# A two-layer hybrid trunk: another order of the seven products in a unit of the up-projections, and the recurrent gates as two steps

## The chip, the cores and the metric

The kernel runs on one core of a Trainium2 chip. The metric is the time of one execution in microseconds of device time; lower is better.

## The reference

1040 tokens (16 learned ones and 1024 of the input) of width 1024 pass through two layers; all of it is float32. Cut to what matters:

```python
def short_conv_mixer(x, w_in, conv_w, w_out):
    h = jnp.einsum('btd,de->bte', x, w_in)            # 1024 -> 3 * 1024
    b_gate, c_gate, v = jnp.split(h, 3, axis=-1)
    u = causal_dwconv(c_gate * v, conv_w)
    return jnp.einsum('btd,de->bte', b_gate * u, w_out)

def rglru_block(x, w_in, conv_w, conv_b, w_gate_a, b_gate_a, w_gate_x, b_gate_x, lam, w_out):
    h = jnp.einsum('btd,de->bte', x, w_in)            # 1024 -> 2 * 1280
    g_branch, r_branch = jnp.split(h, 2, axis=-1)
    gate = jax.nn.gelu(g_branch, approximate=True)
    u = causal_dwconv(r_branch, conv_w) + conv_b      # width 4
    ub = u.reshape(bsz, t_len, RG_BLOCKS, RG_BLOCK_DIM)   # 10 blocks of 128
    r = jax.nn.sigmoid(jnp.einsum('btki,kij->btkj', ub, w_gate_a)... + b_gate_a)
    i = jax.nn.sigmoid(jnp.einsum('btki,kij->btkj', ub, w_gate_x)... + b_gate_x)
    log_a = -RG_C * r * jax.nn.softplus(-lam)
    a = jnp.exp(log_a)
    b = jnp.sqrt(-jnp.expm1(2.0 * log_a)) * (i * u)
    _, hs = lax.associative_scan(_lin_rec_combine, (a, b), axis=1)   # h = a * h + b
    return jnp.einsum('bte,ed->btd', hs * gate, w_out)

def conv_gated_mlp(x, w_up, conv_w, w_down):          # 1024 -> 2 * 2816 -> 1024
    g, v = jnp.split(causal_dwconv(jnp.einsum('btd,df->btf', x, w_up), conv_w), 2, axis=-1)
    return jnp.einsum('btf,fd->btd', jax.nn.silu(g) * v, w_down)

# layer 0: h += short_conv_mixer(rms_norm(h));  h += conv_gated_mlp(rms_norm(h))
# layer 1: h += rglru_block(rms_norm(h));       h += conv_gated_mlp(rms_norm(h))
# out = rms_norm(h)[:, 16:]
```

## The kernel before, in words

Activations lie with the channel in the partitions and the 1040 tokens along the free axis. There are four stages, each an up-projection (`up`) and a down-projection (`down`): the short convolution (sc_w_in, sc_w_out), the first MLP (ffn0), the recurrent block (rg_w_in, rg_w_out) and the second MLP (ffn1). In the profile's span they begin near 0, 391, 1101 and 1483 us; the down-projections begin near 264, 826, 1333 and 1916.

Each float32 operand is split into a high and a low part (`whi`, `wlo` for weights, made by a cast on ACT, L227, and a subtraction on DVE, L228; `zh`, `zl` for the down-projections' activations, L522 and L523), and three products of parts stand for one.

An up-projection works in units. A unit gives two blocks of 128 output channels for all tokens. One unit (two in sc_w_in) is *plain* (L418). Each other one is made in the manner of Strassen and Winograd, of seven products (`product`, L445) of 24 matmuls each, 128 x 128 by 128 x 260, which add up in three banks: bank a takes 1, 6, 7 and 4 one after the other, bank b takes 2, bank c takes 5 and 3. All of PSUM is one pool of four such tiles (`banks`). As a bank is only read between two products that follow each other in it, `take` copies or adds out what it then holds: ACT copies after 1 (L461), 6 (L465), 7 (L468) and 4 (L471), DVE adds after 2 (L463), 7 (L469) and 3 (L473). A product that goes into a bank waits for the copy of the one before it there.

`unit_order` is the hand-written order of TensorE: in a unit 2, 6, 5, 7, then 1 of the next unit (written 1' below), then 4 and 3. After a unit, `finish` does the elementwise part. In the recurrent stage `rg_finish` (one unit is one of the ten blocks) multiplies by the norm (L774, L778) and convolves: an Identity on ACT (L776) and three fused steps on DVE (L624), which give the tile `u`.

The gates of block i (`gates`) run on TensorE one unit later, behind product 3 of unit i + 1: four PSUM tiles, two for the gate `ra` and two for `ix` (L791; each tile is two matmul instructions, and four records in the trace), each followed by a sigmoid on ACT (L794). Then, in the order of the text: GpSimd multiplies ix by u (L795), ACT does tanh (L796), exp (L797), square (L798), sqrt (L800) and gelu (L802), with a table load on ACT wherever the function's table changes, and DVE does L799, L803, the scan (L804) and the product with the gelu (L805), which goes to DRAM (`zrg`). The gates of the last block stand in rg_w_out, after its first pair of output blocks. rg_w_out reads the spilled rows back (`bring`, issued from GpSimd), casts them (L522) and subtracts (L523); DVE evicts its banks at L566.

The order on TensorE and on the DMA queues is that of the code; on ACT and DVE a scheduler with a model of its own sets it, where `tc.high_priority` favours the copies and the sigmoids. Weights are loaded nine pieces and made six pieces ahead of the product that uses them.

## Time and profile before

| | |
|---|---|
| Median of three runs | 2179.39 us (2178.82, 2179.39, 2184.06) |
| The profiled execution | 2182.36 us; its span 2180.5 us |
| TensorE (PE) busy | 2121.6 us, 97% of the span, 17364 matmul records |
| DVE (VectorE) busy | 1489.8 us, 68% |
| ACT (ScalarE) busy | 999.5 us, 46% |
| GpSimd (POOL) busy | 163.5 us, 7% |
| Mean granted clock of TensorE | 0.991 |

All times in the sections below are us from the start of the span. A row of a timeline gives the start, the duration, the engine, the line and the operation, `out<-in`, the sizes, and how many were joined; in brackets the idle time before it and what ended that.

### The profile page before, as it was taken

How to read it: one execution, taken by the hardware profiler on the slowest of the kernel's cores; microseconds unless marked ns; L12 is line 12 of the kernel's file. 1: busy time of each engine (PE TensorE's matmuls, PEld its weight loads, DVE VectorE, ACT ScalarE, POOL GpSimd, SP SyncE). 2: the span in 40 equal slices, each digit the busy share in tenths (PEclk: the TensorE clock that was granted, in tenths of full speed). 3: DMA queues.
4: the chain of work that ended last, by engine and by line, in shares of the span. 5: the costliest groups of instructions: out<-in, count | busy, mean ns of one | idle time of the engine just before them, and what ended most of it. 6: DMA issues, size and time to landing. Idle time of an engine off the chain costs nothing. (4 is left out here: it accounts for less than half of the span.)

```text
span 2180.5 us, 41094 instructions
## 1 busy us (share of the span) xinstructions
PE 2121.6 (97%) x17364; PEld 2108.4 (97%) x17364; DVE 1489.8 (68%) x1858; ACT 999.5 (46%) x1437; POOL 163.5 (7%) x254
## 2 busy tenths in 40 slices
PE   8999999899999999999999999899999999999998
PEld 8999999899999999999989999899999999999997
DVE  8866745887877886233868777497778778763227
ACT  8433433544444444122558788274444444442113
POOL 0000000000000001100001112100000000011002
PEclk9999999999999999999999999999999999999999
DMA  5344454254444446542323345632444444465212
GB/s 179 102 117 113 148 156 118 69 131 117 116 118 120 120 140 205 125 107 65 103 66 93 102 110 151 146 127 68 135 117 114 119 116 122 133 208 148 68 35 78
DMA packets 99545, 257.60 MB, mean 118 GB/s; under 512 B 11040, under 2 KB 19104, under 8 KB 99360
## 3 DMA queue, kind: packets, MB, share of 16 engines
q1 hardware_dynamic: 76320, 172.52, 24.1%
q0 software_dynamic: 22320, 81.73, 18.2%
q8 instruction: 136, 2.23, 0.4%
q10 hardware_dynamic: 720, 0.73, 0.1%
q14 instruction: 49, 0.40, 0.1%
HBM read 205.20 MB, written 49.73 MB: 117 GB/s over the span
## 5 line engine op out<-in xcount | busy, mean ns | idle before, releaser
L445 PE MATMUL ps<-x,whi 128*128 128x260 f32 (+1 forms) x6832 | 1241.7, 284 | 16.6 <-ACT cin L468 8.7
L445 PEld LDWEIGHTS ps<-x,whi 128*128 128x128 f32 x6832 | 1061.9, 190 | 18.7 <-ACT cin L468 9.5
L445 PE MATMUL ps<-x,wlo 128*128 128x260 f32 (+1 forms) x3416 | 969.2, 284 | 0.0
L445 PEld LDWEIGHTS ps<-x,wlo 128*128 128x128 f32 x3416 | 647.5, 190 | 0.0
L556 PE MATMUL ps<-zh,whi 128*128 128x260 f32 (+2 forms) x1888 | 536.1, 284 | 11.4 <-DVE h L566 11.0
L556 PE MATMUL ps<-zl,whi 128*128 128x260 f32 (+2 forms) x1888 | 534.7, 283 | 0.9 <-DVE zl L523 0.9
L556 PE MATMUL ps<-zh,wlo 128*128 128x260 f32 (+2 forms) x1888 | 534.4, 283 | 0.0
L228 DVE TENSOR_TENSOR wlo<-wraw,whi 128x512 fp32r<-128x512 f32 (+1 forms) x337 | 224.8, 671 | 364.7 <-ACT whi L227 364.4
L227 ACT CAST whi<-wraw 128x512 fp32r<-128x512 f32 (+1 forms) x337 | 203.4, 606 | 587.4 <-PE ps L556 347.1
L556 PEld LDWEIGHTS ps<-zh,whi 128*128 128x128 f32 x1888 | 358.2, 190 | 12.8 <-DVE h L566 7.7
L556 PEld LDWEIGHTS ps<-zl,whi 128*128 128x128 f32 x1888 | 358.5, 190 | 1.1 <-DVE zl L523 1.1
L556 PEld LDWEIGHTS ps<-zh,wlo 128*128 128x128 f32 x1888 | 358.2, 190 | 0.0
L227 ACT CAST whi<-s 128x512 fp32r<-128x512 f32 x244 | 150.4, 618 | 258.6 <-PE ps L445 190.2
L624 DVE SCALAR_TENSOR_TENSOR t<-cin,cv,t 128x1040 f32<-128x1040 f32 (+1 forms) x176 | 216.7, 1288 | 5.0 <-ACT t L743 3.3
L228 DVE TENSOR_TENSOR wlo<-s,whi 128x512 fp32r<-128x512 f32 x244 | 166.3, 686 | 44.6 <-ACT whi L227 44.0
L261 POOL DMA_DIRECT2D s<-in_ws x61 | 53.0, 868 | 1241.5 <-DVE cin L740 515.3
L743 ACT ACTIVATE t<-cin,cv 128x1040 f32<-128x1040 f32 (+1 forms) x88 | 97.7, 1152 | 75.5 <-DVE cin L740 75.3
L418 PE MATMUL ps<-x,whi 128*128 128x260 f32 (+1 forms) x640 | 117.1, 285 | 9.2 <-ACT whi L227 9.2
L418 PEld LDWEIGHTS ps<-x,whi 128*128 128x128 f32 x640 | 99.9, 191 | 9.3 <-ACT whi L227 9.2
L740 DVE SCALAR_TENSOR_TENSOR cin<-cin,rn 128x1040 f32<-128x1040 f32 (+1 forms) x88 | 108.1, 1231 | 0.0
L418 PE MATMUL ps<-x,wlo 128*128 128x260 f32 (+1 forms) x320 | 91.1, 285 | 0.1
L463 DVE TENSOR_TENSOR cin<-ps,cin 128x520 f32<-128x520 f32 (+1 forms) x51 | 35.6, 698 | 63.8 <-PE ps L445 63.8
(132 smaller groups left out, 1823.5 us busy)
## 6 DMA issues: line engine op xcount, KB each, us to landing
wraw<-in_ws SPq DMA_DIRECT2D x317, 256.0 KB, 3.5
s<-in_ws SPq DMA_DIRECT2D x61, 512.0 KB, 3.7
s<-in_ws POOLq DMA_DIRECT2D x61, 512.0 KB, 5.7
zff<-t SPq DMA_DIRECT2D x22, 520.0 KB, 2.7
zff<-t SPq DMA_DIRECT2D x22, 512.0 KB, 2.7
h<-h SPq DMA_DIRECT2D x16, 520.0 KB, 2.7
s<-zff POOLq DMA_DIRECT2D x15, 520.0 KB, 4.6
s<-zff POOLq DMA_DIRECT2D x15, 512.0 KB, 4.4
```

The source lines that it names most:

```text
L227: nc.scalar.copy(hi[:, :n], src)
L228: nc.vector.tensor_sub(lo[:, :n], src, hi[:, :n].bitcast(FP32))
L261: nc.gpsimd.dma_start(st["s13"][:, :2 * C], block(q)[:, C:3 * C], accum_op=ALU.add)
L418: nc.tensor.matmul(ps[:, s, :n], lhsT=wt, rhs=x[:, t], start=(j == 0 and k == 0), stop=(j == NJ - 1 and k == 5),)
L445: nc.tensor.matmul(ps[:, b, :n], lhsT=wt[:, c], rhs=x[:, t], start=(first and j == 0 and r == 0), stop=(last and j == NJ - 1 and r == 2), ...
L463: nc.vector.tensor_add(quarter(0, 0), gb, quarter(0, 0))
L556: nc.tensor.matmul(ps[:, s, :n], lhsT=w[wt][:, k], rhs=x[:, t], start=(i == 0 and q == 0), stop=(i == k1 - 1 and q == 2),)
L624: nc.vector.scalar_tensor_tensor(t[:, a:e], cin[:, a + s:e + s], col(wname, at + k), t[:, a:e], op0=ALU.mult, op1=ALU.add)
L740: nc.vector.scalar_tensor_tensor(c, c, sign, rn[:, a:e], op0=ALU.mult, op1=ALU.mult)
L743: nc.scalar.activation(t[:, oa:], cin[:, oa + 2:e + 2], AF.Copy, scale=col(wconv, at + 2))
```

## The change

Three things. `unit_order` becomes 6, 2, 5, 7, 1', 3, 4 (in the first unit 1, 2, 6, 5, 1', 7, 3, 4), so that two products of other banks stand between each pair that follow in bank a. `take` copies bank c after product 5, on ACT, and adds bank a to it after 7, on DVE, where it copied a and added c, both after 7. And the gates of block i become two steps: the one for ra (q = 0) after product 7 of unit i + 1, the one for ix (q = 1) after product 4, followed by `recur`, the elementwise rest as before. The gates of the last block stand after the first and the third pair of rg_w_out.

```diff
 def unit_order(u0, n):
-    out = [(u0, 1)]
+    out = [(u0, 1), (u0, 2)]
     for u in range(u0, n):
-        out += [(u, p) for p in (2, 6, 5, 7)]
-        if u < n - 1:
-            out.append((u + 1, 1))
-        out += [(u, p) for p in (4, 3)]
+        for p in (6, 5, None, 7, 3, 4) if u == u0 else (6, 2, 5, 7, None, 3, 4):
+            if p is not None:
+                out.append((u, p))
+            elif u < n - 1:
+                out.append((u + 1, 1))
     return out
...
             elif p == 6:
                 nc.scalar.copy(quarter(0, 1), ga)
+            elif p == 5:
+                outs[u].append(new_out(u, 1))
+                nc.scalar.copy(quarter(1, 1), gc)
             elif p == 7:
-                outs[u].append(new_out(u, 1))
-                nc.scalar.copy(quarter(1, 1), ga)
-                nc.vector.tensor_add(quarter(1, 1), gc, quarter(1, 1))
+                nc.vector.tensor_add(quarter(1, 1), ga, quarter(1, 1))
...
                 for v in range(n_plain):
-                    between(v)
                     hook(lambda v=v: finish_unit(v))
-            if p == 3:
-                between(u)
+            if p in (7, 4):
+                between(u, p)
+            if p == 4:
                 hook(lambda u=u: finish_unit(u))
...
-    def gates(i, w):
-        u, g = rg.pop(i)
+    def gate(i, q, w):
         n = ALL[1]
-        ra, ix, th = row("ra"), row("ix"), row("th")
-        for q, (bias, got) in enumerate((("b_a", ra), ("b_x", ix))):
-            c = slice(q * P, (q + 1) * P)
-            for b in range(2):
-                ps = banks()
+        u, got = rg[i][0], row(("ra", "ix")[q])
+        rg[i] += (got,)
+        c = slice(q * P, (q + 1) * P)
+        for b in range(2):
+            ps = banks()
...
+        if q:
+            recur(i)
+
+    def recur(i):
+        u, g, ra, ix = rg.pop(i)
+        th = row("th")
         nc.gpsimd.tensor_mul(ix, ix, u)
         nc.scalar.activation(th, ra, AF.Tanh, scale=sp8[:, i:i + 1])
...
+    def gates_between(u, p):
+        add_gate(u - 1, 0 if p == 7 else 1)
+
+    def gates_after(g, m):
+        if g == 0 and m == 0:
+            add_gate(NR - 1, 0)
+        if g == 0 and m == 2:
+            add_gate(NR - 1, 1)
```

The change adds lines, so a line above 70 stands one to seven higher after it (L791 becomes L792, L794 becomes L795, L624 becomes L626). In the lists below the tiles carry the program's numbers, `ps` is a bank, and what an instruction waits for stands in brackets.

**TensorE, at the gates of a steady unit.** Before, behind product 3: four tiles in a row, and the next unit's product 6.

```order
L445 MATMUL ps_13429<-x_12246,wlo_13401 128x260
L791 MATMUL ps_13594<-u_13362,wgate_13325 128x260 [waits DMAHW0_49,PE_49]
L791 MATMUL ps_13594<-u_13362,wgate_13325 128x260
L791 MATMUL ps_13598<-u_13362,wgate_13325 128x260 [waits Activation_49]
L791 MATMUL ps_13598<-u_13362,wgate_13325 128x260
L791 MATMUL ps_13602<-u_13362,wgate_13325 128x260 [waits DVE_49]
L791 MATMUL ps_13602<-u_13362,wgate_13325 128x260
L791 MATMUL ps_13606<-u_13362,wgate_13325 128x260 [waits Activation_49]
L791 MATMUL ps_13606<-u_13362,wgate_13325 128x260
L445 MATMUL ps_13634<-x_11633,whi_13454 128x260 [waits Activation_49]
```

After, behind product 7: the two tiles of ra, and then product 1 of the next unit.

```order
L446 MATMUL ps_13252<-x_12288,wlo_13281 128x260
L792 MATMUL ps_13495<-u_13358,wgate_13228 128x260 [waits DMAHW0_49,DVE_49,PE_49]
L792 MATMUL ps_13495<-u_13358,wgate_13228 128x260
L792 MATMUL ps_13499<-u_13358,wgate_13228 128x260 [waits PE_49]
L792 MATMUL ps_13499<-u_13358,wgate_13228 128x260
L446 MATMUL ps_13512<-x_11627,whi_13364 128x260 [waits Activation_49]
```

The step has halved and moved from behind product 3 of the unit to behind product 7, three products earlier; its first matmul waits for DVE (the tile u), and the product behind it waits for ACT. The two tiles of ix stand behind product 4.

**ACT, around the sigmoids of a steady unit.** Before, from gelu to the casts behind exp and square:

```order
L802 ACTIVATE g_13482<-g_13482 128x1032 [waits DVE_49]
L794 ACT_TABLE_LOAD
L794 ACTIVATE ra_13591<-ps_13594,cv_74 128x520 [waits PE_49]
L794 ACTIVATE ra_13591<-ps_13598,cv_74 128x520 [waits PE_49]
L794 ACTIVATE ix_13592<-ps_13602,cv_74 128x520 [waits PE_49]
L794 ACTIVATE ix_13592<-ps_13606,cv_74 128x520 [waits PE_49]
L796 ACTIVATE th_13593<-ra_13591,sp8_81 128x1040 [waits Activation_49]
L776 ACTIVATE u_13622<-cin_13262,cv_74 128x1040 [waits DMAHW2_49,DVE_49]
L797 ACT_TABLE_LOAD
L797 ACTIVATE ra_13591<-ra_13591,nsp8_82 128x1040 [waits Activation_49]
L227 CAST whi_13630<-wraw_13525 128x512 [waits DMAHW3_49]
L465 COPY cin_13522<-ps_13497 128x2x260 [waits DVE_49,PE_49]
```

After, first from the sigmoids of ix to square:

```order
L795 ACTIVATE ix_13336<-ps_13337,cv_74 128x520 [waits PE_49]
L803 ACTIVATE th_13345<-ra_13234,sp8_81 128x1040 [waits DVE_49,Activation_49]
L795 ACTIVATE ix_13336<-ps_13341,cv_74 128x520 [waits PE_49]
L804 ACT_TABLE_LOAD
L804 ACTIVATE ra_13234<-ra_13234,nsp8_82 128x1040 [waits Activation_49]
L466 COPY cin_13277<-ps_13252 128x2x260 [waits PE_49]
L805 ACTIVATE u_13098<-ra_13234 128x1040 [waits Activation_49,Pool_49]
```

and directly behind, to the sigmoids of ra of the next unit:

```order
L778 ACTIVATE u_13358<-cin_13017,cv_74 128x1040 [waits DMAHW3_49,DVE_49]
L228 CAST whi_13425<-wraw_13309 128x512 [waits DMAHW6_49]
L807 ACT_TABLE_LOAD
L807 ACTIVATE th_13345<-th_13345 128x1040 [waits DVE_49]
L469 COPY g_13454<-ps_13429 128x2x260 [waits PE_49,Activation_49]
L228 CAST whi_13459<-s24_13456 128x512
L228 CAST whi_13490<-wraw_13393 128x512 [waits DMAHW1_49]
L809 ACT_TABLE_LOAD
L809 ACTIVATE g_13194<-g_13194 128x1032
L228 CAST whi_13508<-s13_13245 128x512 [waits DMASW1_49,PE_49]
L795 ACT_TABLE_LOAD [waits DVE_49,PE_49]
L795 ACTIVATE ra_13494<-ps_13495,cv_74 128x520 [waits Activation_49]
```

The four sigmoids stood together, behind gelu of the same block. After, the two of ix are followed by the whole elementwise part with gelu as its last, and the sigmoids of ra of the next block stand behind that; a unit has four table loads before and after. The load ahead of them waited for nothing, and now waits for DVE and TensorE (for the tile u and the first gate tile).

**DVE, from L799 (L806 after) to the convolution of the next block.** Before:

```order
L473 TENSOR_TENSOR cin_13262<-ps_13429,cin_13262 128x2x260 [waits PE_49]
L774 TENSOR_TENSOR cin_13262<-cin_13262,rn_80 128x1040 [waits DVE_49]
L463 TENSOR_TENSOR cin_13522<-ps_13634,cin_13522 128x2x260 [waits PE_49]
L624 SCALAR_TENSOR_TENSOR u_13622<-cin_13262,cv_74,u_13622 128x1040 [waits DMAHW2_49,Activation_49]
L624 SCALAR_TENSOR_TENSOR u_13622<-cin_13262,cv_74,u_13622 128x1040 [waits DVE_49]
L228 TENSOR_TENSOR wlo_13631<-wraw_13525,whi_13630 128x512 [waits DMAHW3_49,Activation_49]
L624 SCALAR_TENSOR_TENSOR u_13622<-cin_13262,cv_74,u_13622 128x1040 [waits DVE_49]
L799 SCALAR_TENSOR_TENSOR th_13593<-u_13362,th_13593 128x1040 [waits Activation_49]
```

After:

```order
L806 SCALAR_TENSOR_TENSOR th_13345<-u_13098,th_13345 128x1040 [waits Activation_49]
L464 TENSOR_TENSOR cin_13277<-ps_13399,cin_13277 128x2x260 [waits PE_49]
L626 SCALAR_TENSOR_TENSOR u_13358<-cin_13017,cv_74,u_13358 128x1040 [waits DMAHW3_49,Activation_49]
L229 TENSOR_TENSOR wlo_13426<-wraw_13309,whi_13425 128x512 [waits DMAHW6_49,Activation_49]
L626 SCALAR_TENSOR_TENSOR u_13358<-cin_13017,cv_74,u_13358 128x1040 [waits DVE_49]
L810 TENSOR_TENSOR ix_13336<-ix_13336,th_13345 128x1040 [waits Activation_49,Pool_49]
L626 SCALAR_TENSOR_TENSOR u_13358<-cin_13017,cv_74,u_13358 128x1040 [waits DVE_49]
L471 TENSOR_TENSOR g_13454<-ps_13252,g_13454 128x2x260 [waits PE_49,Activation_49]
L811 SCALAR_TENSOR_TENSOR th_13345<-ra_13234,ix_13336 128x1040 [waits DVE_49]
```

The convolution's three steps stood ahead of L799 of their unit and now stand behind L806 of it, with the add of product 2 and L810 among them.

## Rows read from the trace of the kernel before

**Rows 1.** Steady unit's window: us; PE, PEld, DVE, ACT, POOL busy; clock, DMA share, GB/s.

```profile
1225.00:1249.66 24.66, 23.96 (x186) 23.14 (x185) 19.20 (x22) 20.11 (x25) 3.41 (x3) 1.00 0.41 102
```

**Rows 2.** Waits of TensorE: total us, times, longest us.

```profile
PE ps L791 <- ACT ra L794: 5.4, 8, 1.0
```

**Rows 3.** Timeline of ACT in a steady unit: start, us, instruction.

```profile
1226.94 0.59 ACT L461 COPY cin<-ps 128x520 f32<-128x520 f32 x1
...
1229.80 0.58 ACT L471 COPY g<-ps 128x520 f32<-128x520 f32 x1
...
1232.44 1.06 ACT L802 ACTIVATE g<-g 128x1032 f32<-128x1032 f32 x1 [0.76 <-DVE g L778]
1233.52 1.28 ACT L794 ACT_TABLE_LOAD   x1
1234.81 1.28 ACT L794 ACTIVATE ra<-ps,cv 128x520 f32<-128x520 f32 x2
...
1238.39 1.25 ACT L776 ACTIVATE u<-cin,cv 128x1040 f32<-128x1040 f32 x1
...
1240.95 1.17 ACT L797 ACTIVATE ra<-ra,nsp 128x1040 f32<-128x1040 f32 x1
1242.02 0.60 ACT L227 CAST whi<-wraw 128x512 fp32r<-128x512 f32 x1
...
1243.02 1.08 ACT L798 ACTIVATE u<-ra 128x1040 f32<-128x1040 f32 x1
```

**Rows 4.** Timeline of TensorE at the gates of two steady units.

```profile
1232.07 2.79 PE L791 MATMUL ps<-u,wgate 128*128 128x260 f32 x12
1235.56 1.14 PE L791 MATMUL ps<-u,wgate 128*128 128x260 f32 x4 [0.70 <-ACT ra L794]
...
1260.22 1.14 PE L791 MATMUL ps<-u,wgate 128*128 128x260 f32 x4 [0.70 <-ACT ra L794]
```

**Rows 5.** Timeline of TensorE: products that waited, at starts and ends of stages.

```profile
258.25 0.50 PE L445 MATMUL ps<-x,whi 128*128 128x260 f32 x2 [1.08 <-ACT c L468]
...
820.79 0.51 PE L445 MATMUL ps<-x,whi 128*128 128x260 f32 x2 [1.95 <-ACT cin L468]
...
1126.34 0.80 PE L445 MATMUL ps<-x,whi 128*128 128x260 f32 x2 [2.78 <-ACT g L468]
...
1323.01 0.51 PE L445 MATMUL ps<-x,whi 128*128 128x260 f32 x2 [0.71 <-ACT g L468]
...
1911.46 0.50 PE L445 MATMUL ps<-x,whi 128*128 128x258 f32 x2 [1.08 <-ACT cin L468]
```

**Rows 6.** Busy time in three windows behind waits (columns as in Rows 1).

```profile
820.80:827.60 6.80, 6.80 (x44) 6.80 (x45) 4.81 (x6) 3.36 (x5) 0.53 (x1) 0.75 0.89 283
1126.40:1129.80 3.40, 3.40 (x17) 3.40 (x18) 3.40 (x4) 2.74 (x3) 0.00 (x0) 0.54 0.02 5
1911.50:1914.90 3.40, 3.40 (x28) 3.40 (x29) 3.40 (x5) 0.99 (x2) 0.41 (x1) 1.00 0.94 225
```

**Rows 7.** Timeline of DVE in the first and in a steady unit.

```profile
1129.83 1.29 DVE L624 SCALAR_TENSOR_TENSOR u<-cin,cv,u 128x1040 f32<-128x1040 f32 x1
...
1240.26 2.63 DVE L624 SCALAR_TENSOR_TENSOR u<-cin,cv,u 128x1040 f32<-128x1040 f32 x2
...
1242.81 0.69 DVE L228 TENSOR_TENSOR wlo<-wraw,whi 128x512 fp32r<-128x512 f32 x1
...
1244.62 1.24 DVE L799 SCALAR_TENSOR_TENSOR th<-u,th 128x1040 f32<-128x1040 f32 x1
```

**Rows 8.** Timeline of rg_w_out: GpSimd's queue, ACT, and TensorE twice.

```profile
1353.19 0.55 POOL L519 DMA_DIRECT2D zs<-zrg  x1 [2.83 <-DVE g L805]
...
1360.73 1.05 ACT L522 CAST zh<-zs 128x1032 fp32r<-128x1032 f32 x1 [4.67 <-DMA zs<-zrg]
...
1369.76 0.58 PE L556 MATMUL ps<-zh,whi 128*128 128x258 f32 x1 [4.50 <-DVE h L566]
...
1388.85 0.45 PE L556 MATMUL ps<-zh,whi 128*128 128x258 f32 x1 [1.96 <-DVE h L566]
```

More of the change, by code (lines that the diff above doesn't have):

```diff
@@ L395, in sum_operands, with up @@
         X[4, j] = split_x(t4, n)
-    def up(name, layer, units, tok, n_plain, new_out, finish, between=lambda u: None, in_last=(), n_late=0, before_pair=lambda j: None, after_plain=lambda js: None):
+    def up(name, layer, units, tok, n_plain, new_out, finish, between=lambda u, p: None, in_last=(), n_late=0, before_pair=lambda j: None, after_plain=lambda js: None):
         a, n = tok
@@ L490, in up @@
         calls = list(in_last)
-        spots = (2, 6, 5, 7, 4, 3)[-len(calls):]
+        spots = (6, 2, 5, 7, 3, 4)[-len(calls):]
         for u, p in unit_order(n_plain, len(units)):
@@ L779, in rg_finish @@
         rg[i] = u, g
-    def gates(i, w):
-        u, g = rg.pop(i)
+    def gate(i, q, w):
         n = ALL[1]
-        ra, ix, th = row("ra"), row("ix"), row("th")
-        for q, (bias, got) in enumerate((("b_a", ra), ("b_x", ix))):
-            c = slice(q * P, (q + 1) * P)
-            for b in range(2):
-                ps = banks()
-                for s in range(2):
-                    t = slice((2 * b + s) * n, (2 * b + s + 1) * n)
-                    nc.tensor.matmul(ps[:, s, :n], lhsT=w[:, c], rhs=u[:, t], start=True, stop=True)
-                t = got[:, 2 * b * n:2 * (b + 1) * n].rearrange("p (s n) -> p s n", s=2)
-                with tc.high_priority():
-                    nc.scalar.activation(t, ps[:, :, :n], AF.Sigmoid, bias=col(bias, i))
+        u, got = rg[i][0], row(("ra", "ix")[q])
[3 more added lines that the diff above has]
+            ps = banks()
+            for s in range(2):
+                t = slice((2 * b + s) * n, (2 * b + s + 1) * n)
+                nc.tensor.matmul(ps[:, s, :n], lhsT=w[:, c], rhs=u[:, t], start=True, stop=True)
+            t = got[:, 2 * b * n:2 * (b + 1) * n].rearrange("p (s n) -> p s n", s=2)
+            with tc.high_priority():
+                nc.scalar.activation(t, ps[:, :, :n], AF.Sigmoid, bias=col(("b_a", "b_x")[q], i))
+        if q:
[3 more added lines that the diff above has]
+        th = row("th")
         nc.gpsimd.tensor_mul(ix, ix, u)
@@ L806, in gates, with add_gate @@
         nc.sync.dma_start(zd1[i][:, a:], g[:, a:])
-    def add_gates(i):
-        step((gate_pieces[i],), lambda w: gates(i, w))
+    def add_gate(i, q):
+        if 0 <= i < NR:
+            step((gate_pieces[i],), lambda w: gate(i, q, w))
+    def gates_between(u, p):
[5 more added lines that the diff above has]
+            add_gate(NR - 1, 1)
     mixer_then(
@@ L813, in trunk_kernel @@
         ("rg_w_out", 0, RG_GROUPS, zd1, TAIL, lambda m: hd[1][m], next_operands(hd[2], TAIL, "g_ffn1")),
-        extra={"between": lambda u: add_gates(u - 1) if u else None},
-        at=lambda g, m: add_gates(NR - 1) if (g, m) == (0, 0) else None,
+        extra={"between": gates_between},
+        at=gates_after,
     )
```

## The prediction

> **What bounds the kernel now.** I read the waits of TensorE first, then the timelines of the recurrent stage, because both halves of the change meet there. TensorE is busy nearly always, so the time is its work plus its gaps, and the change leaves its work alone: same products, same gate matmuls. Everything below is therefore about gaps. In a steady unit of the recurrent stage one window of 24.66 us has ACT busy for 20.11 us [rows 1], so ACT's order can decide when a bank comes free. The gates' matmuls wait for ACT's sigmoid of a gate tile 5.4 us in all [rows 2]: the fourth gate tile finds no bank until the first tile's sigmoid is done. The period shows it: the same row stands at 1235.56 and 1260.22 [rows 4], 24.66 us apart. Seven products at 2.87 us (two copies that each follow a product are 2.86 us apart [rows 3]) are 20.09, and 16 gate records at 0.22 us (12 records took 2.79, the last 0.15 of it running out [rows 4]) are 3.52; 24.66 - 23.61 = **1.05 us of gap in each unit**.
>
> **The change part by part.** *New product order, ends of stages.* Outside the recurrent stage I see no gap in the middle of the stages; gaps stand at last units, where product 4 follows 7 in bank a with no product of a next unit between, and waits for the copy: 1.08, 1.95, 0.71 and 1.08 us [rows 5]. After, product 3 stands between 7 and 4: 2.87 us of cover against at most 1.95. All four go, 4.82 us. The clock was at 0.75 of its full level for 6.8 us behind the second gap, and at 1.00 behind the one of 1.08 [rows 6]; 6.8 x 0.25 = 1.7 us go with it. Together **-6.5**. In mid-stage the order swaps which copy is awaited, but every follower in a bank has two products (5.7 us) between, so I cost that at nothing; if a copy came more than 5.7 us late, the excess would show once in each unit.
>
> *Gates of a steady unit (seven of them, u = 2 to 8).* Let G be the end of the unit's second gate step. Four products (6, 2, 5, 7) follow, to G + 11.47; then the first gate step of the next unit wants two things.
>
> First, the convolved tile u. DVE runs L806, the add of product 2, convolution, wlo, convolution, L810, convolution (third order fence). Its start hangs on ACT: ACT starts a sigmoid some 1.1 us behind a gate tile's first matmul, so the first ix sigmoid starts at G - 0.64; then sigmoid, tanh and sigmoid, load, exp, copy, square. With 0.64 us a sigmoid, 1.28 a load, 1.17 an exp (tanh alike), 0.58 a copy and 1.08 a square [rows 3], less 0.1 of overlap each, square ends near G + 5.6. DVE from there: L806 1.24 (L799 before), the add 0.69 (as wlo), three convolutions of 1.31, wlo 0.69, and L810 1.24 (as L799) [rows 7], less 0.1 of overlap each: 7.3, to **G + 12.95**. TensorE stalls 1.5 us there. Before, the same convolution had two more products of time.
>
> Second, a bank for product 1 of the next unit: a and c still hold sums (c has 5, a has 7), so the first gate step takes the two free banks and product 1 must wait for the first **ra sigmoid**. On ACT that now stands behind all of recur, gelu last: after square come Identity (1.25), a cast (0.60), load, sqrt (1.08), a copy, two casts, load, gelu (1.06) and a cast (second order fence; durations [rows 3]), to about G + 14.0. Then comes the sigmoid's table load, and the wait for the gate's own matmuls stands ahead of that load: with u at 12.95, the first tile reaches ACT near G + 14.1. Load and sigmoid end near **G + 16.1**, and the gate's matmuls (8 x 0.22) at 14.7: product 1 stalls about 1.4 us. Both ways to the sigmoid meet there, so this stall has a floor: 1.1 + 1.28 + 0.64 - 1.76, some 1.3 us, even with an idle ACT. Before, the load stood ahead of the wait and cost nothing.
>
> Sum 2.95 against 1.05, seven times: **+13.3**. Each us more on the chain to u costs 7 us.
>
> Each table load stands as 1.28 us, and the sigmoid behind it starts 0.01 us after its end (1233.52 + 1.28 = 1234.80 against 1234.81 [rows 3]). The Trainium skill (ScalarE: Activation LUTs, What ACT_TABLE_LOAD costs) speaks against this part of the change more strongly: about 1.38 us of drain on top of 1.28 for every switch of set. The trace does not agree: the load at 1233.52 starts 0.02 us behind the end of gelu (1232.44 + 1.06) and its follower directly behind it. By the page the four loads of a unit would put the sigmoid 5.5 us later, an estimate, and the unit's gap at 8.4 instead of 2.95: 2224 us instead of 2185.3 below.
>
> *First unit of the recurrent stage.* The first gate step of unit 0 now comes after product 7 of unit 1, and needs the plain unit's convolution. That hangs on DVE, where its third convolution ended at 1129.83 + 1.29 = 1131.12 [rows 7], behind the norm's reciprocals, which the change doesn't touch. The products 1, 2, 6, 5, 1', 7 are done at 1126.34 - 2.78 = 1123.56 (the start of the waiting product, less its gap [rows 5]). So a stall of 7.6 us takes the place of 2.78, of the slow clock behind it (3.4 us at 0.54: 1.6 [rows 6]) and of some 1.05 us at its gates. After the longer stall I take 1.6 to 3 us of slow clock, and no second gap for the unit. 9.4 (8.6 to 10.6) against 5.4: **+4** (3 to 5).
>
> *Ends of the stage.* Gates 8 wait for their convolution as the others (+1.5), and at the start of rg_w_out the fourth bank waits for an ix sigmoid behind a cast of zh (+1.6, by the same durations; 0 if that sigmoid is early): **+3.1**.
>
> *rg_w_out.* Two gaps stand there, 4.50 and 1.96 us, both behind an eviction on DVE that is queued behind zl, zl behind zh on ACT, and zh behind the reload of zrg [rows 8]; the reload was issued at 1353.19, behind g's product, which the last gates feed. With the slow clock behind each (3.3 and 1.6 by the dip of [rows 6], twice as long for the first) that is some 11.4 us. After, the last gates are split over (0, 0) and (0, 2), and the scan of the unit before comes earlier against the products, so I read the reload about 5 us earlier in POOL's order. 4.50 goes, part of the second may stay: **-8**; bounds 0 (the reload waits as long as now) and -11.4.
>
> **The sum** against the profiled execution, 2182.36 us: -6.5 + 13.3 + 4 + 3.1 - 8 = +5.9, 2188.3. The median of the runs is 2179.39, 2.97 below it: **2185.3 us**. A measurement here tells about 0.3%, 6.5 us, from no change, so the forecast stands just inside the edge of slower (2185.9).
>
> **The rivals.**
> *The convolved tile is in time* (the other side). If the chain to u were 1.5 us shorter than I sum (the copy or the square earlier, L810 behind the last convolution), the first stall goes in seven units and at gates 8: -12.0; the last scans then come earlier as well, and the second gap of rg_w_out goes with the first, -3.4. Point of decision: u ends before G + 11.5. 2185.3 - 15.4 = **2169.9**. Against it: the order puts L806 and L810 between the convolutions, and both hang on ACT. 0.13.
> *The slow clock comes into every unit.* The two stalls are 1.5 and 1.4 us with only 1.76 us of gate matmuls between; behind 1.95 the clock fell, behind 1.08 not [rows 5, 6]. 1.6 us in each of seven units: 2185.3 + 11.2 = **2196.5**. 0.11.
> *The reload stays late* in rg_w_out (the change doesn't do there what the order promises): 2185.3 + 8 = **2193.3**. 0.14.
>
> **How the numbers follow.** The forecast has the remaining 0.62, with a range of its own of 2180 to 2191 from the bounds of the first unit (1), the ends of the stage (1.6) and rg_w_out (3.4 the one way). I split it 0.35 within 0.3% (up to 2185.9) and 0.27 slower. Faster: 0.13. Same: 0.35. Slower: 0.27 + 0.11 + 0.14 = 0.52. The range leaves out half of the case at 2169.9, the clock's and a little at each end of the forecast: 2170 to 2195, with 0.8 in it.
>
> **What would show it.** Right: waits of gate matmuls for DVE's convolution (about 1.5 us) and of product 1 for the ra sigmoid (about 1.4), eight or nine times each, and a period near 26.5 us in the stage; no gap left at 820.79's place and its three likes; one gap of 7 to 8 us at the first unit; no 4.50 in rg_w_out. Wrong: a period of 23.6 to 24.7, the tile u ready when TensorE asks for it, a clock below 1 in the steady units, or the reload still behind the casts.

## The result, and the profile after

The changed kernel takes 2230.1 us (median of four runs, 2229.49 to 2232.62) against 2179.2 of the kernel before: a ratio of 1.0227, with an interval of 1.0214 to 1.0240, some 49 us slower. Its profiled execution took 2230.61 us with a span of 2228.7, 48.25 more than the one of before. The forecast was 2185.3 us, and 2195 the upper end of its range.

Where the time went is seen from stage to stage. The table gives the time in us from the first matmul of a stage's half to the first of the next (in the last row to the last matmul), from the traces; e18, e13 and e14 are experiments told below.

| | before | after | e18 | e13 | e14 |
|---|---|---|---|---|---|
| sc_w_in | 255.0 | 264.3 | 252.0 | 255.8 | 257.2 |
| sc_w_out | 100.5 | 99.5 | 99.9 | 100.6 | 99.5 |
| ffn0 up | 463.5 | 463.5 | 458.7 | 460.4 | 461.1 |
| ffn0 down | 253.1 | 254.7 | 254.3 | 254.3 | 254.2 |
| rg_w_in and gates | 251.2 | 285.1 | 274.6 | 273.8 | 247.4 |
| rg_w_out | 130.3 | 130.8 | 131.4 | 130.5 | 129.3 |
| ffn1 up | 454.6 | 457.0 | 452.7 | 452.8 | 452.7 |
| ffn1 down, end | 254.2 | 255.3 | 254.2 | 254.1 | 254.1 |

The recurrent stage's up-projection lost 33.9 us, and that of the first stage, which has no gates at all, 9.3. The waits of TensorE after (total us, times, longest us) begin:

```profile
PE ps L792 <- issue: 20.5, 9, 6.8
PE ps L345 <- DVE tt L338: 15.3, 4, 6.6
PE ps L419 <- ACT whi L228: 9.2, 1, 9.2
PE ps L558 <- DVE h L568: 8.4, 5, 2.8
PE ps L446 <- DVE wlo L229: 7.3, 1, 7.3
PE ps L446 <- ACT ra L795: 6.9, 7, 1.2
```

The first row is the gates' wait for the tile u (the profile found no releaser; the order in the section on the change names DVE), the last product 1's wait for the ra sigmoid: both forecast. The second and the fifth were not: the norm's matmuls wait for `tt`, and once a product waits for a weight's low part. In the kernel before no product waited for a low part, and the wait for `tt` was

```profile
PE ps L344 <- DVE tt L337: 5.3, 4, 2.5
```

Behind both stands one instruction of DVE. Product 6 takes its weights from a sum (`s24`, L271): piece 1 plus a staged tile `s13`, which a load on SP's queue and an accumulating transfer on GpSimd's queue fill. The group of this line, after and then before (busy us, mean ns | idle of DVE ahead of it, and what ended it):

```profile
L271 DVE TENSOR_TENSOR s<-s,wraw 128x512 f32<-128x512 f32 x61 | 42.5, 697 | 91.2 <-DMA s<-in_ws 88.0 <-DMA wraw<-in_ws 3.2
```

```profile
L270 DVE TENSOR_TENSOR s<-s,wraw 128x512 f32<-128x512 f32 x61 | 41.8, 686 | 17.3 <-DMA s<-in_ws 14.1 <-DMA wraw<-in_ws 3.2
```

DVE stood still for 88 us until that transfer landed, where it had been 14. At the norm of the recurrent stage (timelines of DVE and TensorE, after):

```profile
1120.85 0.68 DVE L229 TENSOR_TENSOR wlo<-wraw,whi 128x512 fp32r<-128x512 f32 x1
1128.89 0.69 DVE L271 TENSOR_TENSOR s<-s,wraw 128x512 f32<-128x512 f32 x1 [7.37 <-DMA s<-in_ws]
1129.50 0.69 DVE L338 TENSOR_TENSOR tt<-rn,tt 128x520 fp32r<-128x520 f32 x1
...
1130.25 1.02 PE L345 MATMUL ps<-tt,ones 128*128 128x260 f32 x3 [6.64 <-DVE tt L338]
```

The sum stands ahead of `tt` in DVE's queue, waits 7.37 us, and the norm's matmuls wait 6.64 for something that had nothing to do with the transfer. In the kernel before the sum stood ahead of `tt` at this place too, and did not wait, because the load into `s13` was issued earlier. DVE and SP's queue (SPq), before:

```profile
1099.68 0.68 DVE L228 TENSOR_TENSOR wlo<-s,whi 128x512 fp32r<-128x512 f32 x1
1111.65 0.69 DVE L270 TENSOR_TENSOR s<-s,wraw 128x512 f32<-128x512 f32 x1
1113.51 0.70 DVE L337 TENSOR_TENSOR tt<-rn,tt 128x520 fp32r<-128x520 f32 x1 [0.44 <-PE ps L344]
...
1100.39 0.33 SPq L260 DMA_DIRECT2D s<-in_ws  x1
```

and after:

```profile
1115.67 0.69 DVE L229 TENSOR_TENSOR wlo<-s,whi 128x512 fp32r<-128x512 f32 x1 [0.31 <-ACT whi L228]
...
1116.39 0.33 SPq L261 DMA_DIRECT2D s<-in_ws  x1
```

The stage's first matmul ran at 1081.30 before and at 1091.17 after, so the load follows it by 19.1 and by 25.2 us. In both it is issued 0.03 us behind the end of the low part (`wlo<-s`) that is made from the old contents of `s13`. That tile has one buffer; piece 1' refills it, and the weights of product 7 are its last reader. With 1' ahead of 7 in the order of the pieces, 7 is made one piece later.

The 7.3 us of the first stage are a product 6 that waits for the low part of its weights, which is made from the sum. DVE waited 3.62 us for that sum's transfer, and then stood at the norm's and the convolution's work for some 18 us before it came to the low part. In steady units it is the convolution that stands behind the sum:

```profile
1214.46 1.24 DVE L780 SCALAR_TENSOR_TENSOR g<-g,rn 128x1040 f32<-128x1040 f32 x1
1220.05 0.69 DVE L271 TENSOR_TENSOR s<-s,wraw 128x512 f32<-128x512 f32 x1 [4.36 <-DMA s<-in_ws]
1220.78 0.69 DVE L272 TENSOR_TENSOR s<-s,wraw 128x512 f32<-128x512 f32 x1
1221.38 1.24 DVE L806 SCALAR_TENSOR_TENSOR th<-u,th 128x1040 f32<-128x1040 f32 x1
...
1227.32 1.30 DVE L626 SCALAR_TENSOR_TENSOR u<-cin,cv,u 128x1040 f32<-128x1040 f32 x1
```

The gates of two units in a row, on TensorE (the rows that answer to [rows 4]), and their windows (columns as in [rows 1]):

```profile
1201.09 1.99 PE L792 MATMUL ps<-u,wgate 128*128 128x260 f32 x8 [1.32 <-issue]
...
1204.32 0.51 PE L446 MATMUL ps<-x,whi 128*128 128x260 f32 x2 [1.23 <-ACT ra L795]
...
1228.72 2.95 PE L792 MATMUL ps<-u,wgate 128*128 128x260 f32 x8 [2.20 <-issue]
...
1232.05 0.80 PE L446 MATMUL ps<-x,whi 128*128 128x260 f32 x2 [0.38 <-ACT ra L795]
```

```profile
1200.00:1226.70 26.70, 24.20 (x184) 23.19 (x184) 18.36 (x21) 19.87 (x26) 3.41 (x3) 1.00 0.36 89
1226.70:1254.30 27.60, 25.20 (x183) 23.90 (x184) 20.09 (x22) 19.36 (x26) 3.43 (x3) 0.94 0.37 93
```

Where u is late by 1.32 us of idle the unit lasts some 26.7 us; where the sum adds to it (2.20), the gates run at a lower clock (8 records in 2.95 us, against 1.99) and the unit lasts about 27.6. The first gate step of the stage waited 6.84 us, forecast as 7.6. In rg_w_out the reload of zrg was issued at 1396.41, landed 9 us later, and held the casts, `zl` and the eviction at 1411.11 as in [rows 8], now with a gate matmul behind them:

```profile
1396.41 0.56 POOL L521 DMA_DIRECT2D zs<-zrg  x1 [1.28 <-issue]
...
1405.38 1.06 ACT L524 CAST zh<-zs 128x1032 fp32r<-128x1032 f32 x1 [10.02 <-DMA zs<-zrg]
...
1406.47 1.23 DVE L525 TENSOR_TENSOR zl<-zs,zh 128x1032 fp32r<-128x1032 f32 x1 [8.54 <-ACT zh L524]
...
1411.86 3.84 PE L792 MATMUL ps<-u,wgate 128*128 128x260 f32 x8 [3.81 <-DVE h L568]
```

### The profile page after: what moved, and what is told of

The parts are those of the page before. It is cut to its first block, busy times and chain, and to the rows that moved or that the text cites. A ratio compares the mean times of both kernels' runs of the same rounds, so it can differ in the third digit from the quotient of the medians.

```text
span 2228.7 us, 41009 instructions
## 1 busy us (share of the span) xinstructions
PE 2134.0 (96%) x17364; PEld 2116.7 (95%) x17364; DVE 1478.8 (66%) x1858; ACT 994.8 (45%) x1438; POOL 160.7 (7%) x254
## 5 line engine op out<-in xcount | busy, mean ns | idle before, releaser
L558 PEld LDWEIGHTS ps<-zh,whi 128*128 128x128 f32 x1888 | 357.0, 189 | 12.9 <-issue 5.3
L626 DVE SCALAR_TENSOR_TENSOR t<-cin,cv,t 128x1040 f32<-128x1040 f32 (+1 forms) x176 | 226.3, 1289 | 50.5 <-ACT t L745 46.6
L271 DVE TENSOR_TENSOR s<-s,wraw 128x512 f32<-128x512 f32 x61 | 42.5, 697 | 91.2 <-DMA s<-in_ws 88.0
```

Of the source, the lines that this page charges most:

```text
L271: nc.vector.tensor_add(s24[:, :C], st["s13"][:, :C], st[11])
L558: nc.tensor.matmul(ps[:, s, :n], lhsT=w[wt][:, k], rhs=x[:, t], start=(i == 0 and q == 0), stop=(i == k1 - 1 and q == 2),)
L626: nc.vector.scalar_tensor_tensor(t[:, a:e], cin[:, a + s:e + s], col(wname, at + k), t[:, a:e], op0=ALU.mult, op1=ALU.add)
```

## The experiments

Ratios are to the kernel before on the same chip; "us" is the ratio less one, times 2179.

**The parts by halves: e1 and e2.** e1 is the changed kernel with its gates as one step; e2 the kernel before with the gates split.

```diff
 # e1, of the changed kernel
-        add_gate(u - 1, 0 if p == 7 else 1)
+        if p == 4:
+            add_gates(u - 1)          # gate(i, 0, w); gate(i, 1, w) in one step
 # e2, of the changed kernel: unit_order and take of before, and
-            if p in (7, 4):
+            if p in (7, 3):
                 between(u, p)
```

> The changed kernel with its order of products and its copies, but the gates of a block as one step again, behind product 4. Theory 1 (two separate losses: the order makes the staged weight sum of product 6 come late, which costs about 21 us outside the steady recurrent units; the split of the gates costs about 27 us from the first gates to the end of the recurrent stage): about 2203 us, the period of a recurrent unit at or below 24.7 us, the long norm gaps (6.9, 4.5, 4.2 us) and the 7.5 us wait in the first stage still there. Rival (the late weight sum, at the head of DVE's queue, is also what delays the gates): 2215 us or more, the period above 26.

> The kernel before with its order of products and its copies; only the gates are two steps, ra behind product 7 and ix behind product 3. Theory 1: 2200 to 2206 us, all of the loss between the first gates and the end of the recurrent stage, norm gaps as before. Rival: about 2185 us, since without the late weight sum the tile u is in time and only the wait for the ra sigmoid is left.

Measured: e1 1.0137 (1.0121 to 1.0154), +30 us; e2 1.0051 (1.0036 to 1.0066), +11 us. Both came out between their two expectations. So the order, not the gates, carries most, and 8 us arise only from both together. In e2 the gates' rows are

```profile
1203.68 1.92 PE L790 MATMUL ps<-u,wgate 128*128 128x260 f32 x8
...
1206.84 0.51 PE L445 MATMUL ps<-x,whi 128*128 128x260 f32 x2 [1.25 <-ACT ra L793]
```

u is in time there, and the wait for the ra sigmoid is left. In e1 the norm gaps and the 7.3 us wait of the first stage stand as in the changed kernel, as theory 1 had it, but the period is also 24.4 to 27.7 us: the late sum reaches the recurrent units too, as the rival had it.

**Other places: e3 and e4.**

```diff
 # e3
-        for p in (6, 5, None, 7, 3, 4) if u == u0 else (6, 2, 5, 7, None, 3, 4):
+        for p in (6, 5, 7, None, 3, 4) if u == u0 else (2, 6, 5, 7, None, 3, 4):
 # e4
-            if p in (7, 4):
+            if p in (3, 4):
                 between(u, p)
```

> The changed kernel with two exchanges in its order: 2 before 6 in each unit, and 7 before 1' in the first unit of a stage; the gates as in the changed kernel. Theory 1: the staged sum has its one product of lead back, DVE's wait for it falls from 88 us to about 14, the norm gaps and the 7.5 us wait go: 2203 to 2210 us. Rival (the norm gaps come from the copies that moved between ACT and DVE): within 5 us of the changed kernel's 2230.

> The changed kernel with the ra gates behind product 3 in place of 7; product 4 behind them needs no new bank, and u has two more products of time. Theory 1: both waits of a steady unit go, period near 23.7 to 24.5 us, 2200 to 2207 us. Rival (the bank wait only moves to the ix gates, because the ra sigmoid is behind gelu on ACT anyway): 2218 us or more.

Measured: e3 1.0164 (1.0143 to 1.0186), +36 us: the norm gaps of the recurrent stage and of ffn1 went, but DVE's wait for the sum stayed near 77 us and the first stage lost 22 us. e4 1.0153 (1.0137 to 1.0168), +33 us, between the two expectations; its periods lie between 25.2 and 28.3 us. So e3 fits theory 1 (the number of products between the release of s13 and the sum decides) at the starts of these two stages, where 7 is ahead of 1' again, and not elsewhere: it came out between its two expectations as well.

**One part of the order alone, on the kernel before: e5 to e8.**

```diff
 # e5: take of the change (copy of c behind 5, add of a behind 7), order of before
 # e6
-        out += [(u, p) for p in (4, 3)]
+        out += [(u, p) for p in (3, 4)]
 # e7, in all units but the first
-        out += [(u, p) for p in (2, 6, 5, 7)]
+        out += [(u, p) for p in (6, 2, 5, 7)]
 # e8, in the first unit alone: 1, 2, 6, 5, 1', 7, 3, 4
```

> The kernel before with one part of the change: take copies bank c behind product 5 and adds bank a behind 7. Order of products and gates as before. Theory 1 (the late sum for product 6 comes from the order of the pieces): within 4 us of the kernel before. Theory 2 (it comes from the copy of 5 and the row that it takes one product earlier, which the GpSimd queue and ACT wait for): 10 to 20 us slower, with DVE's wait for the staged sum above 40 us.

> The kernel before with one part of the change: product 3 ahead of 4 in each unit, the gates as one step behind 4. Theory 1: the waits of the last units go and nothing else moves: 2173 to 2179 us. Theory 3 (it is this swap that makes the sum late, since it alone separates the changed kernel's second variant from the order before): 10 to 20 us slower, mostly in the first stage and in the recurrent one.

> The kernel before with one part of the change: 6 ahead of 2 in each unit but the first of a stage. Theory 1: this takes one of five products from the way between the release of the staged tile and the sum: 10 to 20 us slower, DVE's wait for the staged sum above 40 us. Theories 2 and 3: within 4 us of the kernel before.

> The kernel before with one part of the change: the first unit of a stage in the order 1, 2, 6, 5, 1', 7, 3, 4. Theory 1: the staged tile comes free one product later at the start of each stage: the norm gaps of 6 to 8 us and the 7.5 us wait of the first stage stand here, 8 to 18 us slower. Theories 2 and 3: within 4 us of the kernel before.

Measured: e5 +11 us (1.0052, 1.0037 to 1.0067), e6 +52 (1.0240, 1.0223 to 1.0257), e7 +4 (1.0017, 1.0007 to 1.0026), e8 +29 (1.0132, 1.0117 to 1.0148). They are no sum of the change, since order and copies belong together: with the old copies product 3 must wait for the add into bank c behind 7, and with the new ones 4 for the add of bank a. Theory 1 failed for e7 (10 to 20 us forecast), and for e8 it held with more than the 8 to 18 us that it gave: the norm's matmuls wait 14.7 us there, and the load into s13 comes 25.2 us behind the first matmul of the recurrent stage, as in the changed kernel. Theory 2 had the size of e5 but not the way, since DVE waits 21 us there for the sum and not above 40; theory 3 had 10 to 20 us for e6. The waits of TensorE in e5, and in e6:

```profile
PE ps L445 <- DVE cin L470: 15.8, 5, 4.3
```

```profile
PE ps L446 <- DVE g L470: 19.4, 9, 4.6
PE ps L446 <- DVE cin L470: 16.9, 5, 4.3
```

What e6 showed beyond that is DVE's order. There the sum (L271 in e6) stands ahead of the convolution; in the kernel before it stood behind it. Both from the programs, e6 first:

```
L779 SCALAR_TENSOR_TENSOR g_13222<-g_13222,rn_80 128x1040 [waits Activation_49]
L271 TENSOR_TENSOR s24_13490<-s13_13227,wraw_13225 128x512 [waits DMASW1_49,DVE_49]
L272 TENSOR_TENSOR s24_13490<-s24_13490,wraw_13368 128x512 [waits DMAHW1_49,DVE_49]
L464 TENSOR_TENSOR cin_13262<-ps_13374,cin_13262 128x2x260 [waits PE_49]
L625 SCALAR_TENSOR_TENSOR u_13362<-cin_13002,cv_74,u_13362 128x1040 [waits DMAHW4_49,Activation_49]
```

```
L624 SCALAR_TENSOR_TENSOR u_13362<-cin_13002,cv_74,u_13362 128x1040 [waits DVE_49]
L799 SCALAR_TENSOR_TENSOR th_13333<-u_13102,th_13333 128x1040 [waits Activation_49]
L228 TENSOR_TENSOR wlo_13401<-s24_13230,whi_13400 128x512 [waits Activation_49]
L228 TENSOR_TENSOR wlo_13455<-wraw_13368,whi_13454 128x512 [waits DMAHW1_49,PE_49,Activation_49]
L270 TENSOR_TENSOR s24_13490<-s13_13227,wraw_13225 128x512 [waits DMASW1_49,DVE_49]
```

s24 is one buffer, and the weights of product 3 are its last reader (`wlo_13401<-s24_13230`). With 4 ahead of 3 that reader came last, and kept the sum late in DVE's order; with 3 ahead of 4 the scheduler could put the sum earlier than its transfer lands. That was theory 4. It is a second way to the same wait: at the starts of the stages the transfer comes later, in the steady units the sum stands earlier.

**The sum held back: e9 to e11.** e9 is e6, e10 the changed kernel and e11 is e3, each with one write more:

```diff
-            return split_weights(src, C)
+            made = split_weights(src, C)
+            if p == 4:
+                nc.vector.tensor_copy(st["s24"][:, 2 * C:2 * C + 1], made[1][:, :1].bitcast(FP32))
+            return made
```

> Product 3 ahead of 4 as in the run before of that part alone (52 us slower than the kernel before), with one thing more: making the weights of piece 4 also writes one unused column of the staging tile s24, so that the sum for product 6 can't be written before piece 4 is made. Theory 4 (with 3 ahead of 4 the tile s24 comes free one piece earlier, the scheduler puts the sum earlier in DVE's queue than its transfer lands, and DVE waits with everything behind it): the loss goes, 2173 to 2181 us, DVE's wait for the staged sum below 20 us. Rival (the number of products between the release of s13 and the sum decides, which the extra column doesn't change): within 6 us of 2232.

> The changed kernel with the same extra write in piece 4. Theory 4: the steady units lose their waits for the staged sum, the starts of the stages keep theirs (1' ahead of 7 in the first unit) and the split gates theirs: 2203 to 2218 us, the unit's period in the recurrent stage at most 26.6. Rival: within 6 us of the changed kernel's 2230.

> The variant of the changed kernel with 2 ahead of 6 and 7 ahead of 1' (2216 us), with the same extra write. Theory 4: only the split gates (11 us by themselves) and the moved copies (11 us) are left, less the 6 us of the last units: 2190 to 2200 us. Rival: within 6 us of 2216.

Measured: e9 1.0105 (1.0091 to 1.0119), +23 in place of +52; e10 1.0186 (1.0169 to 1.0202), +41 in place of +49; e11 1.0049 (1.0032 to 1.0066), +11 in place of +36. One unused column is worth 29, 9 and 25 us. e11 came as expected. e9 stayed above its expectation although DVE's wait for the sum fell from 85 to 16 us, and keeps 26.8 us of waits for the adds that its old copies cause. e10 missed its range too, above it, but the steady units came as theory 4 had them: their sums no longer wait, and the gates stand 26.74 us apart in unit after unit. What is left stands in the first stage and at the starts of the others, where 1' is still ahead of 7. DVE's group, the waits of TensorE, and the gates of two units in e10:

```profile
L271 DVE TENSOR_TENSOR s<-s,wraw 128x512 f32<-128x512 f32 x61 | 42.0, 688 | 43.9 <-DMA s<-in_ws 40.1 <-DMA wraw<-in_ws 3.1
```

```profile
PE ps L348 <- DVE tt L341: 14.2, 4, 5.4
PE ps L449 <- DVE wlo L229: 7.2, 1, 7.2
```

```profile
1200.73 1.99 PE L795 MATMUL ps<-u,wgate 128*128 128x260 f32 x8 [1.31 <-issue]
...
1227.47 1.99 PE L795 MATMUL ps<-u,wgate 128*128 128x260 f32 x8 [1.31 <-issue]
```

**The last units: e12 and e15.**

```diff
 # e12: only for the last unit of a stage
-        out += [(u, p) for p in (4, 3)]
+        out += [(u, p) for p in ((4, 3) if u < n - 1 else (3, 4))]
 # e15: e12, with the new copies in that unit
+            elif p == 5 and u == len(units) - 1:
+                outs[u].append(new_out(u, 1))
+                nc.scalar.copy(quarter(1, 1), gc)
+            elif p == 7 and u == len(units) - 1:
+                nc.vector.tensor_add(quarter(1, 1), ga, quarter(1, 1))
```

> The kernel before with product 3 ahead of 4 in the last unit of each stage alone, where no unit follows whose sum could come early. Theory 4 and the step of the prediction on the ends of the stages: the four waits of the last units go: 2172 to 2176 us. Rival (the last units' waits only move to the down-projection's first matmuls): 2178 to 2181 us.

> The kernel before with 3 ahead of 4, the copy of c behind 5 and the add of a behind 7 in the last unit of each stage alone (the run of the last unit without those copies lost 12 us, since product 3 then follows 7 directly and waits for its copy and its add). If that is the cause, the last units' waits go now: 2171 to 2177 us. If the waits only move on: 2179 or more.

Measured: e12 1.0055 (1.0042 to 1.0068), +12 us, against both of its expectations: the four waits of 4 (4.8 us in all) turned into longer ones of 3 for the add, 11.0 us in all (two of them in the row below), with a lower clock behind three of them.

```profile
PE ps L445 <- DVE cin L469: 6.8, 2, 3.6
```

e15 0.9976 (0.9967 to 0.9985), 5 us faster; its four waits are gone.

**TensorE's order kept, the pieces in the old order: e13 and e14.** The loads, sums and splits of weights go by a list of pieces; here it has the order of before (2, 6, 5, 7, 1', 4, 3), while TensorE's instructions are those of the changed kernel (e13) or of e1 (e14), one for one. How far loads and splits run ahead is counted by the list too; that part of the edit is left out here.

```diff
+            in_order.extend(pieces[u][p] for u, p in piece_order(n_plain, len(units)))
...
+        spots = [k for k, p in enumerate(pieces) if p in in_order]
+        for k, p in zip(spots, in_order):
+            pieces[k] = p
```

> The changed kernel with the same order on TensorE, instruction for instruction, and the same gates; only the pieces of weights are loaded, summed and split in the order of the kernel before (2 ahead of 6, 7 ahead of 1', 4 ahead of 3). Theory 4 (the loss outside the gates is that of the order in which weights are made: the staged sum for product 6 stands in DVE's queue ahead of its transfer): 2190 to 2202 us, DVE's wait for the staged sum below 25 us, no norm gap above 6 us. Rival (TensorE's order itself: copies and adds that come late for the product behind them): above 2220.

> The variant with the changed order and copies and the gates as one step (2209 us), with the pieces of weights made in the order of the kernel before, and TensorE's order untouched. Theory 4: the loss of 29 us goes and the gain of the last units stands: 2172 to 2180 us. Rival: above 2200.

Measured: e13 1.0085 (1.0072 to 1.0099), +19 us, and in the table all of it in the recurrent stage; e14 0.9968 (0.9956 to 0.9981), 7 us faster than the kernel before, as expected, and the fastest version here. Its period is 24.42 us, against 24.66, with a wait of 0.46 where [rows 4] have 0.70:

```profile
1205.21 2.79 PE L813 MATMUL ps<-u,wgate 128*128 128x260 f32 x12
1208.46 1.14 PE L813 MATMUL ps<-u,wgate 128*128 128x260 f32 x4 [0.46 <-ACT ra L816]
```

DVE still waits 35 us for the sum in e13, above what was expected, but all of it but 0.7 us in the first stage, which takes 255.8 us against 255.0 before.

**The transfer taken away: e18.**

```diff
-                nc.vector.tensor_add(s24[:, :C], st["s13"][:, :C], st[11])
+                nc.vector.tensor_add(s24[:, :C], st[11], st[11])
```

> The changed kernel, whose sum for product 6 is built from piece 1 twice and leaves out the staged part s13, so that DVE's instruction needs no transfer by the accumulating queue; everything else as in the changed kernel, and s13 still used for products 5 and 7. Theory 4 in its narrow form (DVE's wait for that transfer, at the head of its queue, is the loss outside the gates): 2198 to 2208 us. If the order of the pieces costs by itself in other ways (the splits that stand later, the release of s13): 2212 to 2230.

Measured: 1.0075 (1.0059 to 1.0092), +16 us in place of +49, as the narrow form had it. The order of instructions on TensorE is that of the changed kernel, and on DVE too but for some forty of 1858, so that little else changed with the transfer. The sum's group, the wait for `tt`, and the gates of two units:

```profile
L271 DVE TENSOR_TENSOR s<-wraw 128x512 f32<-128x512 f32 x61 | 41.7, 684 | 3.2 <-DMA wraw<-in_ws 3.0
```

```profile
PE ps L345 <- DVE tt L338: 2.2, 4, 0.6
```

```profile
1203.48 1.99 PE L792 MATMUL ps<-u,wgate 128*128 128x260 f32 x8 [1.32 <-issue]
...
1206.71 0.51 PE L446 MATMUL ps<-x,whi 128*128 128x260 f32 x2 [1.24 <-ACT ra L795]
...
1230.22 1.99 PE L792 MATMUL ps<-u,wgate 128*128 128x260 f32 x8 [1.32 <-issue]
```

Each unit is now like the next, 26.74 us apart, with 1.6 us from the last product to the gates where 0.12 is the pitch, and 1.62 from the gates to product 1 where theirs is 0.22.

**The two waits of the split gates: e16 and e17.**

```diff
 # e16, of the changed kernel
-        nc.scalar.activation(g[:, a:], g[:, a:], AF.Gelu_apprx_tanh)
+        nc.scalar.activation(g[:, a:], g[:, a:], AF.Sigmoid)
 # e17, of e13
-            if p in (7, 4):
+            if p in (3, 4):
                 between(u, p)
```

> The changed kernel with a sigmoid in place of gelu in the recurrent stage, which changes that part of the computation: the ra sigmoid then needs no table load of its own behind its matmuls. If product 1 waits for that load and the sigmoid, as the prediction has it (1.3 to 1.6 us a unit): 2214 to 2221 us and no wait of product 1 above 0.5 us in a steady unit. Rival (the wait is ACT's queue ahead of the sigmoid): within 4 us of 2230, the wait still near 1.6.

> The changed order and copies, with the pieces of weights made in the order of the kernel before, and the ra gates behind product 3 in place of 7: u has two products more, and product 4 behind the gates needs no new bank. If the split gates lose only by their place, both waits of a steady unit (1.55 and 1.62 us with the ra gates behind 7) go, the period falls to 23.7 to 24.2 us, and the time to 2165 to 2172, below the 2174 of the one-step gates. Rival (the ix gates then wait for a bank or for the ra sigmoid behind gelu instead): a period above 25 and 2180 to 2195.

Measured: e16 1.0209 (1.0195 to 1.0223), +46 us, between its two expectations. The wait of product 1 for the ra sigmoid (6.9 us) is gone from the list, as expected, but the gates' wait for u rose from 20.5 to 24.0 us: half of what the one gave was taken there.

```profile
1201.13 1.99 PE L792 MATMUL ps<-u,wgate 128*128 128x260 f32 x8 [1.75 <-issue]
...
1228.49 3.80 PE L792 MATMUL ps<-u,wgate 128*128 128x260 f32 x8 [3.21 <-issue]
```

e17 1.0008 (0.9998 to 1.0018), the same as before and 17 us better than with the ra gates behind 7. It missed its range all the same (2165 to 2172 us), and its period of 25.0 to 25.3 us and its time are those of the rival. The two waits are gone, and another has come: the second ra tile waits 1.07 to 1.38 us in each unit for DVE's add of product 3, whose bank it takes.

```profile
1209.64 1.14 PE L813 MATMUL ps<-u,wgate 128*128 128x260 f32 x4 [1.07 <-DVE cin L495]
```

## Why the prediction was wrong, by its own steps

**The step that failed** is the one on the new order in mid-stage: "every follower in a bank has two products (5.7 us) between, so I cost that at nothing". It looked at the banks, and they did not lose. But the order of products is also the order in which weights are loaded, summed and made, and through the sum for product 6, which the prediction left out of every chain, that cost some 33 us. It did so in two ways. At the starts of the stages 1' ahead of 7 frees s13 one piece later, the transfer lands later, and the sum waits with the norm behind it; of the norm's reciprocals the prediction said that the change doesn't touch them. In the steady units the sum stands earlier in DVE's queue, ahead of L806 and the convolution on which the prediction counted.

e18 measures both together: of the 49 us, 33 go with the transfer. Some 3 of these are waits that the kernel before had as well (`tt` 5.3 us before, 2.2 in e18). e13 says the same from the other side, 31 us. By place, most of it lies at the starts: `tt` and the low part cost TensorE 20.4 us more in the changed kernel than in e18, with a lower clock behind each gap (0.72 over the 6.8 us behind the one of 6.64). The steady units lost little: six of them, from the gates at 1174.35 to those at 1338.16, take 163.8 us, and 160.5 in e18.

**Steady gates**: right in mechanism and nearly in size. Without the late sum (e18) the two gaps are 1.6 and 1.62 us by starts, 1.48 and 1.40 above the pitches, against 1.5 and 1.4 forecast, and the period 26.74 against 26.56 (24.66 + 1.9). Both waits are the named ones: with u in time (e2) only the second stands, with no table load (e16) the second goes. The chain to u is right as well: in e18 the ix gates start at 1188.70 and end, by 8 x 0.22 us, at 1190.46, and the last step of the convolution ends 12.9 us later, forecast as 12.95.

```profile
1202.09 1.29 DVE L626 SCALAR_TENSOR_TENSOR u<-cin,cv,u 128x1040 f32<-128x1040 f32 x1
```

The durations that it names, less 0.1 each, put the end of the square at 5.3 us and not at the 5.6 that it gives and e18 has; nothing overlaps at a table load [rows 3].

**First unit**: 7.6 forecast, 6.84 of idle measured after and 7.67 in e18. The stage in e18 has +23.5 us in all, where the terms of the steady units, the first unit and gates 8 add up to 18.8. Most of the 4.7 between is the slow clock. Behind the long stall it stood at 0.52 for 6.8 us, which is 3.3 us where the forecast took 1.8, with a second gap of 0.79 in the gates where it took none. Behind the wait of gates 8, 1.93 us, it stood at 0.75 for 6.8 us, 1.7 us for which no term stood (both from e18, columns as in [rows 1]):

```profile
1123.90:1130.70 6.80, 5.98 (x19) 4.71 (x20) 0.00 (x0) 1.39 (x2) 0.86 (x1) 0.52 0.48 107
1337.80:1344.60 6.80, 6.78 (x36) 6.23 (x37) 6.20 (x7) 4.74 (x6) 1.12 (x2) 0.75 0.34 93
```

**The clock** fell in every second unit or so of the changed kernel; that rival was real in part, and the late sum brought it about, since e10, e13 and e18 have the full clock (1.00) in the steady units.

**Ends of stages**: the four waits went, but only together with the copies (e12 against e15). They are worth 5 us in e15 and were forecast at 6.5; in the changed kernel the late sums ate them (ffn0 unchanged, ffn1 2.4 slower, and in e18 4.8 and 1.9 faster). A part moved on: the first matmuls of the MLPs' down-projections wait 1.15 and 1.05 us there for the copy of 4.

**rg_w_out**: -8 was wrong, and the third rival right: the reload left 20.2 us behind the start of the half, as before (20.7), and rg_w_out takes 130.8 us against 130.3. That the reload would come 5 us earlier was read from the order on GpSimd; what held it there the profile doesn't name (`issue`), and it stays open.

**The Trainium skill's rule** (ScalarE: Activation LUTs, What ACT_TABLE_LOAD costs) of 1.38 us more for a table load: the traces don't agree. In e18 the load at 1201.68 starts 0.02 us behind the cast ahead of it, and the steady gates fit the sum without the drain. That the 2224 us by that rule lie near the measured 2230 is chance, since the loss was not at the loads.

The way from 2185.3 to 2230.1 is thus: 33 us of the sum's transfer, 8 of rg_w_out, and the rest in the main in the recurrent stage. What stays open is how the 33 us divide between 1' ahead of 7, 6 ahead of 2 and 3 ahead of 4, the more so in the first stage; the three depend on each other (e3, e10 and e11), and no run has one of them alone with the new copies. That the scheduler reckons the accumulating transfer shorter than it is was not measured; its placing of the sum was only seen.

## What to carry to other kernels

When the order of one engine's work is changed, follow every list that is made from that order: here the loads, sums and splits of weights moved with the products, and the banks, which the change was about, were not where the time went. In each in-order queue look for the instruction that waits for a transfer, at what a scheduler has put behind it, and at what frees the buffer that the transfer fills; a wait of 4 to 7 us there reached engines that need nothing of the transfer. If an order is good for one resource and bad for another, separate the two (e14: TensorE in the new order, weights in the old one, 7 us faster than the kernel before).

## What the runs showed that was not expected

A write of one unused column, a dependency and no work, was worth 9 to 29 us (e9 to e11), by moving the sum in DVE's order. The single-buffered tile s24 had kept the sum late enough in the kernel before; freeing it earlier made the kernel slower. The other one, s13, worked the other way: freed later, it made its transfer late. And of the two waits of the split gates the second could be taken away with little gain while the sum was late (e16), and both only with a smaller wait in their place (e17).
